# A mixture-of-experts stage: late loads, the place of a branch, gathers by chunk, routing in token halves

## The chip, the core and the metric

One core of a Trainium2 chip runs the whole program. The metric is the device time of one execution in microseconds. TensorE (PE) multiplies matrices and transposes, VectorE (DVE), ScalarE (ACT) and GpSimd (POOL) do the elementwise work, and SyncE (SP) issues nearly all transfers. All numbers are float32.

## The reference

Two transformer blocks follow each other on 256 tokens of width 1024. The first block's mixture of experts is where the change lies:

```python
logits = (xt @ w_router + b_router)                     # 256 x 32
top_vals, top_idx = lax.top_k(logits, 4)
gates = softmax(top_vals)
# for each token and each of its 4 experts e:
hgu  = xb @ w_up_gate[e] + b_up_gate[e]                 # 1024 x 2048
glu  = minimum(hgu[:, :1024], 7.0); lin = clip(hgu[:, 1024:], -7, 7)
hact = glu * sigmoid(1.702 * glu) * (lin + 1.0)
y   += gate * (hact @ w_down[e] + b_down[e])            # 1024 x 1024
# then, on the same rows (ple):
gate = sigmoid(rmsnorm(x) @ w_ple_gate)
x    = x + (p @ w_ple_proj) * gate
```

Ahead of it stand two kinds of attention (`mixer`), behind it a second block (`mixer2`, `ffn2`).

## The kernel before

`moe` keeps both blocks of 128 tokens in `xt` and gives each expert 64 slots. `route` computes the logits, the top 4 of each token and its slot in each expert (`posm`). `turn_half` transposes half of the columns of `xt` for both token blocks into `rT`, by `turn_quarter`; the products with `wr` (L1070) stand in `p4`, go to `l4`, and are turned to tokens in `pr` (L1078). VectorE finds the top 4 (L1085 to L1094), a product with a triangle (`pp`, L1097) counts the slots. `route` is a generator, whose parts `moe` takes one at a time.

For each group of four experts, `select` writes the selection matrix `S` from `posm`, and `gather` multiplies the normalized tokens `hn` with it, chunk by chunk of 128 columns, into `XST`, the experts' inputs, transposed. For each expert `up` multiplies them with the up and gate weights (8 loads of 1 MB, L830), `act` turns the result and applies bias and activation, and `down` multiplies with the down weights (4 loads of 1 MB, L864). `combine_weights` and `combine` bring pairs of experts back to the tokens and add them to `xt`. The loop runs `up(ex)`, then `down(ex - 1)`, so that `act` has time. The orders of PE and of SP in this stage are written out by hand (`manual_schedule`); the other engines are ordered by a planner.

The weights go through 20 buffers of 1 MB: two rings of five, five of the six `g` buffers of the pool `big` (`g3` holds `rT` and later every second `XST`), and `ring3` of five. `self.order` lists them in the order of their use; `raw()` takes the next one. SP issues the loads in program order, and a load waits until the buffer's last reader is done. At expert 20 `retire` is set: when `g0` is next, `ple_proj` takes `g0`, `g1` and `g5` out of the order for what ple needs, and loads `p` and `w_ple_proj`. Its products come as a generator, `extra`, one step behind an `up` or at the end of an expert.

64 slots may be too few for an expert. Then `flag` is 1 and `more_tokens` runs all experts over all tokens in a loop; with these inputs the branch (L976) skips it. It stands between experts 28 and 29. Each engine loads the flag into a register (L975) and branches by itself.

`ple` follows the last expert: `ahead_of` loads the first half of `w_ple_gate` and splits it into two float32r parts (`whi` on ACT, L155, `wlo` on DVE, L156), `feat` transposes `xt` (`tr_m`, L248), and `lin` multiplies (L201 to L203).

Of the kernel before, what the change touches and what calls it, by code (L numbers as in the profile page):

```python
# [10 lines left out]
F32 = mybir.dt.float32  # L11
# [25 lines left out]
RING3 = 5  # L37

# [53 lines left out]
class Net:  # L92
# [640 lines left out]
    def moe(self, stop=None):  # L733
# [4 lines left out]
        with ExitStack() as es:  # L738
# [20 lines left out]
            route = self.route(b1, b2, p_h, p_y, p_m, gates, gT, posm, iota, bT, flag)  # L759
            S, SG, XST, CG, Y, H, U = {}, {}, {}, {}, {}, {}, {}  # L760
            extra = []

# [16 lines left out]
            def gather(g, k2, first=False):  # L779

                flat = lambda t: t.rearrange("p e s -> p (e s)")
                ps = None if first else p_m.tile([P, 2, G, SLOTS], F32, name="pg", tag="m")
                for kk in range(2):
                    k = 2 * k2 + kk
                    o = p_m.tile([P, G, SLOTS], F32, name="pg1", tag="m") if first else ps[:, kk]
                    for b in range(2):
                        nc.tensor.matmul(flat(o), hn[:, b, blk(k)], flat(S[g][b]), start=b == 0 and (first or kk == 0), stop=b == 1, skip_group_check=True)  # L787
                    if first:
                        turn_out(g, k, o, kk)
                if not first:  # L790
                    if k2 % 2:
                        gain = self.gc[:, GFFN + 2 * k2:GFFN + 2 * k2 + 2].unsqueeze(2).to_broadcast([P, 2, G * SLOTS])
                        nc.vector.tensor_tensor(XST[g][:, 2 * k2:2 * k2 + 2].rearrange("p k e s -> p k (e s)"), ps.rearrange("p k e s -> p k (e s)"), gain, op=ALU.mult)
                    else:
                        for kk in range(2):
                            turn_out(g, 2 * k2 + kk, ps[:, kk], 0)
# [59 lines left out]
            def down(ex):  # L856

                hT = H.pop(ex)
                py = p_y.tile([P, 512], F32, name="py", tag="y")
                for k in range(8):  # L860
                    if k % 2 == 0:
                        raw = self.rows_of(a["w_down"][0, ex][k * P:k * P + 256], 2)
                    for n in range(2):
                        nc.tensor.matmul(py[n * 64:n * 64 + 64], hT[:, k], raw[:, k % 2, half(n)], start=k == 0, stop=k == 7, skip_group_check=True)  # L864
                if ex % 2 == 0:
                    Y[ex // 2] = b1.tile([P, 2, 512], F32, name="yy")
                y = Y[ex // 2][ex % 2 * 64:ex % 2 * 64 + 64]
                nc.scalar.copy(y[:, 0], py[0:64])  # L868
                nc.vector.tensor_copy(y[:, 1], py[64:128])

            def down_bias():

                for n in range(2):
                    for b in range(2):
                        po = p_m.tile([P, 512], F32, name="pbd", tag="m")
                        nc.tensor.matmul(po, gT[:, blk(b)], bd[:, half(n)], start=True, stop=True)
                        s = xt[:, b, half(n)]
                        nc.vector.tensor_tensor(s, s, po, op=ALU.add)
# [10 lines left out]
            with tc.manual_schedule(engines={mybir.EngineType.PE, mybir.EngineType.SP}):  # L889
# [4 lines left out]
                gather(0, 0, True)  # L894
# [31 lines left out]
            self.more_tokens(flag, posm, gates, hn, b1, b2, p_up, p_m)  # L926
            with tc.manual_schedule(engines={mybir.EngineType.PE, mybir.EngineType.SP}):
                for ex in range(29, 32):
                    up(ex)
                    if ex == 31:  # L930
                        act(ex)
                    down(ex - 1)
                    if ex < 31:
                        act(ex)
                    if ex == 30:
                        combine(14)
# [8 lines left out]
    def ple_proj(self, p_m):  # L945

        nc, a = self.nc, self.a
        self.retire = None
        self.pj = self.big.tile([P, 2, D], F32, name="pj", tag="g0")
        p = self.big.tile([P, 4, 512], F32, name="p", tag="g1")  # L950
        p, pT = (p[:, i].rearrange("p (b d) -> p b d", b=2) for i in range(2))
        self.order = [o for o in self.order if o[1] not in ("g0", "g1", "g5")]
        nc.sync.dma_start(p, a["p"][0, 0].rearrange("(b p) d -> p b d", p=P))
        raw = self.rows_of(a["w_ple_proj"][0], 2)

        def steps():
# [12 lines left out]
            yield  # L969
        return steps()  # L970

    def more_tokens(self, flag, posm, gates, hn, b1, b2, p_up, p_m):
# [3 lines left out]
        with tc.If(more > 0):  # L976
# [5 lines left out]
            ha = b1.tile([P, 8, T], F32, name="ha", tag="xst")  # L982
# [48 lines left out]
    def turn_quarter(self, n, b, pool, tag):  # L1031
# [5 lines left out]
        nc.vector.tensor_copy(self.rT[:, 4 * n:4 * n + 4, blk(b)], ps)  # L1037

    def route(self, b1, b2, p_h, p_y, p_m, gates, gT, posm, iota, bT, flag):
        nc, a, tc, xt = self.nc, self.a, self.tc, self.xt  # L1040
        with ExitStack() as es:
# [22 lines left out]
            for n in range(2):  # L1064
                if n == 1:
                    for b in range(2):
                        self.turn_quarter(1, b, p_m, "m")
# [6 lines left out]
            l4 = b1.tile([P, T], F32, name="l4", tag="SG0")  # L1074
            nc.vector.tensor_copy(l4, p4)
# [19 lines left out]

            pp = p_m.tile([P, 2, 32], F32, name="pp", tag="m")
# [17 lines left out]

            pb = p_y.tile([P, 4, P], F32, name="pb", tag="y")
            for c in range(4):
                nc.tensor.transpose(pb[:, c], braw[:, blk(c)], self.ident)
            nc.scalar.copy(bT, pb)
            pgt = p_m.tile([32, T], F32, name="pgt", tag="m")
            for b in range(2):  # L1120
                nc.tensor.transpose(pgt[:, blk(b)], gates[:, b], self.ident)
            nc.scalar.copy(gT, pgt)
# [666 lines left out]
```

## Time and profile before

| what | value |
|---|---|
| time, median of 3 runs | 1584.93 us (1582.86 to 1586.02) |
| time of the profiled execution | 1583.55 us |
| its span, first to last instruction | 1581.7 us |
| TensorE busy | 1477.2 us (93%) |
| VectorE, ScalarE, GpSimd busy | 657.1, 457.2, 103.0 us |
| moved by DMA | 499.51 MB, mean 316 GB/s |
| mean granted TensorE clock | 0.993 of full |

The profile is one execution. The share of busy time is a mean over stages with different limits; of a stage one asks what its last wait is for. The granted clock is the part of full speed (2.4 GHz) that TensorE was given in a stretch; 0.50 is 1.2 GHz. Lines are those of the kernel before.

### The profile page before, as it was taken

What the parts mean: (1) busy time and instruction counts of PE and PEld (TensorE: products, weight loads), DVE (VectorE), ACT (ScalarE), POOL (GpSimd) and SP (SyncE); (2) the same over time, 40 slices, a digit from 0 to 9 for tenths busy, and PEclk for the clock granted to TensorE, in tenths of its full rate; (3) what the DMA queues carried; (4) which work ended last, traced back from release to release, by engine and by line L of the source; (5) the groups of instructions that cost most, each with busy time, mean ns of one, the idle gap of its engine ahead of it and who ended that gap; (6) DMA issues with size and microseconds to landing.
All of it is one profiled execution on the core that took longest, in us unless ns stands there. A gap on an engine that the chain in (4) does not pass through costs nothing. (4 is left out here: it accounts for less than half of the span.)

```text
span 1581.7 us, 19461 instructions
## 1 busy us (share of the span) xinstructions
PE 1477.2 (93%) x7671; PEld 839.9 (53%) x7671; DVE 657.1 (42%) x1200; ACT 457.2 (29%) x849; POOL 103.0 (7%) x213
## 2 busy tenths in 40 slices
PE   8999999999998988988998988788999999999998
PEld 6776433333332332332332332222797779899986
DVE  6666313231322222221311231122789657676654
ACT  7655101110100100100110100001677565464443
POOL 3220000000000000000000000000306100000000
PEclk9999999999999999999999999899999999999999
DMA  8737799999999999999999999999354224656651
GB/s 271 299 132 285 284 411 424 423 421 424 423 421 424 423 422 423 424 422 422 392 381 422 421 423 421 421 375 416 129 196 147 81 94 160 195 165 187 187 192 48
DMA packets 135873, 499.51 MB, mean 316 GB/s; under 512 B 12355, under 2 KB 36291, under 8 KB 103011
## 3 DMA queue, kind: packets, MB, share of 16 engines
q1 hardware_dynamic: 135299, 497.31, 79.9%
q8 instruction: 62, 1.02, 0.3%
q10 hardware_dynamic: 480, 0.92, 0.2%
q14 instruction: 32, 0.26, 0.0%
HBM read 497.15 MB, written 1.05 MB: 315 GB/s over the span
## 5 line engine op out<-in xcount | busy, mean ns | idle before, releaser
L830 PE MATMUL pu<-raw,xst 128*64 128x512 f32 x2048 | 459.2, 599 | 26.0 <-DMA raw<-in_w_up_gate_dram 19.5
L830 PEld LDWEIGHTS pu<-raw,xst 128*64 128x64 f32 x2048 | 141.2, 137 | 325.9 <-issue 266.7
L864 PE MATMUL py<-raw,hT 128*64 128x512 f32 x1024 | 238.9, 599 | 40.7 <-DMA raw<-in_w_down_dram 40.5
L156 DVE TENSOR_TENSOR wlo<-raw,whi 128x1024 fp32r<-128x1024 f32 (+2 forms) x178 | 214.9, 1211 | 121.0 <-ACT whi L155 120.6
L155 ACT CAST whi<-raw 128x1024 fp32r<-128x1024 f32 (+2 forms) x178 | 181.0, 1022 | 171.0 <-PE pt_lin L229 83.5
L833 DVE COPY u<-pu 128x512 f32<-128x512 f32 x32 | 22.1, 691 | 419.4 <-PE pu L830 419.4
L229 PE MATMUL pt_lin<-xl,whi 128*128 128x256 f32 x640 | 180.4, 284 | 0.0
L228 PE MATMUL pt_lin<-xh,whi 128*128 128x256 f32 x640 | 179.8, 285 | 0.6 <-ACT xh L257 0.6
L230 PE MATMUL pt_lin<-xh,wlo 128*128 128x256 f32 x640 | 178.7, 283 | 0.4 <-DVE wlo L156 0.4
L864 PEld LDWEIGHTS py<-raw,hT 128*64 128x64 f32 x1024 | 69.5, 136 | 206.1 <-issue 145.8
L846 DVE TENSOR_TENSOR h<-ph,bT 128x512 f32<-128x512 f32 x64 | 44.1, 689 | 256.3 <-PE ph L843 255.5
L832 ACT COPY u<-pu 128x512 f32<-128x512 f32 x32 | 18.8, 586 | 391.1 <-PE pu L830 391.1
L228 PEld LDWEIGHTS pt_lin<-xh,whi 128*128 128x128 f32 x640 | 120.2, 189 | 4.6 <-issue 3.3
L230 PEld LDWEIGHTS pt_lin<-xh,wlo 128*128 128x128 f32 x640 | 120.4, 189 | 4.1 <-issue 3.1
L229 PEld LDWEIGHTS pt_lin<-xl,whi 128*128 128x128 f32 x640 | 121.0, 189 | 2.7 <-issue 2.6
L868 ACT COPY yy<-py 64x512 f32<-64x512 f32 x32 | 18.5, 579 | 280.7 <-PE py L864 280.7
L885 PE MATMUL po<-yy,cg 128*128 128x512 f32 x128 | 62.8, 614 | 9.7 <-DVE xt L887 9.0
L787 PE MATMUL pg<-S,hn 128*128 128x256 f32 x256 | 63.7, 394 | 0.9 <-DVE S L770 0.9
L850 ACT ACTIVATE sg<-h 128x256 f32<-128x256 f32 x64 | 26.7, 417 | 124.2 <-DVE h L848 124.2
L776 POOL TENSOR_TENSOR SG<-S,gates 128x256 f32<-128x256 f32 x16 | 10.9, 703 | 718.1 <-DVE h L848 712.1
L202 PE MATMUL ps_lin<-wlo,xh 128*128 128x512 f32 (+1 forms) x144 | 56.5, 396 | 0.6 <-DVE wlo L156 0.6
L203 PE MATMUL ps_lin<-whi,xl 128*128 128x512 f32 (+1 forms) x144 | 55.4, 389 | 0.0
(449 smaller groups left out, 1744.2 us busy)
## 6 DMA issues: line engine op xcount, KB each, us to landing
raw<-in_w_up_gate_dram SPq DMA_DIRECT2D x256, 1024.0 KB, 19.5
raw<-in_w_down_dram SPq DMA_DIRECT2D x138, 1024.0 KB, 19.7
raw<-in_w_in_dram SPq DMA_DIRECT2D x33, 1024.0 KB, 5.2
raw<-in_w_gate_up_dram SPq DMA_DIRECT2D x44, 512.0 KB, 4.9
raw<-in_w_out_dram SPq DMA_DIRECT2D x8, 1024.0 KB, 13.4
raw<-in_w_ple_gate_dram SPq DMA_DIRECT2D x4, 1024.0 KB
raw<-in_w_ssd_proj_dram SPq DMA_DIRECT2D x4, 1024.0 KB, 4.9
raw<-in_w_in_dram SPq DMA_DIRECT2D x4, 512.0 KB
```

What stands on the lines that cost most here:

```text
L155: a = self.nc.scalar.copy(hi, src)
L156: b = self.nc.vector.tensor_tensor(lo, src, f32(hi), op=ALU.subtract)
L202: nc.tensor.matmul(ps[b][:, :n], xh[:, k, xs], lo[:, c, :n], start=False, stop=False)
L203: i = nc.tensor.matmul(ps[b][:, :n], xl[:, k, xs], hi[:, c, :n], start=False, stop=k == nk - 1)
L228: nc.tensor.matmul(o, hi[:, c, cs], xh[:, k, :], start=k == 0 and j % 2 == 0, stop=False, skip_group_check=True)
L229: nc.tensor.matmul(o, hi[:, c, cs], xl[:, k, :], start=False, stop=False, skip_group_check=True)
L230: nc.tensor.matmul(o, lo[:, c, cs], xh[:, k, :], start=False, stop=k == nk - 1, skip_group_check=True)
L787: nc.tensor.matmul(flat(o), hn[:, b, blk(k)], flat(S[g][b]), start=b == 0 and (first or kk == 0), stop=b == 1, skip_group_check=True)
L830: nc.tensor.matmul(ps[j][q * 64:q * 64 + 64], xst[:, k, i], raw[:, half(2 * q + j)], start=k == 0, stop=k == 7, skip_group_check=True)
L846: nc.vector.tensor_tensor(h, ph, bT[:, :, o:o + 3:2].unsqueeze(3).to_broadcast([P, 4, 2, SLOTS]), op=ALU.add)
L864: nc.tensor.matmul(py[n * 64:n * 64 + 64], hT[:, k], raw[:, k % 2, half(n)], start=k == 0, stop=k == 7, skip_group_check=True)
L885: nc.tensor.matmul(po, CG[c][:, blk(b)], Y[c][:, n], start=True, stop=True)
```

## The change

- **Routing in token halves**: the second half of the columns is transposed, multiplied and copied for one block of 128 tokens after the other; the copies of the second block are shared by ACT and DVE.
- **Between the top 4 and the slot count** PE gets the transposes of the up bias (`braw`), which stood behind `up(0)`, and four products (`WARM`) whose result nobody reads.
- **Gathers by chunk**: group 0 gathers two chunks ahead of `up(0)` (four before) and one chunk ahead of each of its products 1 to 6 (two chunks ahead of two of them before). `combine_weights(0)`, `select(1)` and `gather(1, 0)` move from behind `act(0)` into expert 1, and the rest of group 1's gathers into experts 2 and 3.
- **Late loads into retired slots**: `w_ple_proj` goes to `g5`, `p` to `g1`, `b_down` to a free part of `g1`. `b_down` was loaded ahead of the experts, its product with the gates (`down_bias`) stood behind `act(0)`; both move to `ple_proj`, as two more steps.
- **The branch** moves from between experts 28 and 29 to behind the last `combine`; behind the first products of `down(31)` PE is given a hint that it will be taken. The tile `ha` of the skipped part moves to `g3`.

```diff
@@ moe
-            gT = b1.tile([32, T], F32, name="gT", tag="cg2")
-            bd = b1.tile([32, D], F32, name="bd", tag="yy")
-            nc.scalar.dma_start(bd, a["b_down"][0])
...
+            def gather1(k):
+
+                o = p_m.tile([P, G, SLOTS], F32, name="pg1", tag="m")
+                for b in range(2):
+                    nc.tensor.matmul(flat(o), hn[:, b, blk(k)], flat(S[0][b]), start=b == 0, stop=b == 1)
+                turn_out(0, k, o, k % 2)
...
-                        nc.tensor.matmul(py[n * 64:n * 64 + 64], hT[:, k], raw[:, k % 2, half(n)], start=k == 0, stop=k == 7, skip_group_check=True)
+                        i = nc.tensor.matmul(py[n * 64:n * 64 + 64], hT[:, k], raw[:, k % 2, half(n)], start=k == 0, stop=k == 7, skip_group_check=True)
+                    if k == 0:
+                        self.mm = i.ins
...
                 select(0)
-                gather(0, 0, True)
+                gather1(0)
+                gather1(1)
                 next(route)
                 select_gates(0)
 
-                up(0, lambda k: gather(0, k // 2 + 1, True) if k in (0, 2, 4) else None)
+                up(0, lambda k: gather1(k + 1) if 0 < k < 7 else None)
                 next(route)
                 act(0)
-                down_bias()
-                combine_weights(0)
-                select(1)
-                gather(1, 0)
-                for ex in range(1, 29):
+                for ex in range(1, 32):
                     g, i = ex // G, ex % G
                     if ex == 20:
-                        self.retire = lambda: extra.append(self.ple_proj(p_m))
+                        self.retire = lambda: extra.append(self.ple_proj(p_m, gates))
                     up(ex)
                     if extra:
                         next(extra[0], None)
+                    if ex == 31:
+                        act(ex)
                     down(ex - 1)
-                    act(ex)
+                    if ex < 31:
+                        act(ex)
+                    if ex == 1:
+                        combine_weights(0)
...
-                        if i == 0:
+                        if i == (1 if g == 0 else 0):
                             select(g + 1)
-                        gather(g + 1, i)
+                        for k2 in [i] if g else {1: [0], 2: [1], 3: [2, 3]}[i]:
+                            gather(g + 1, k2)
...
-            self.more_tokens(flag, posm, gates, hn, b1, b2, p_up, p_m)
-            with tc.manual_schedule(engines={mybir.EngineType.PE, mybir.EngineType.SP}):
-                for ex in range(29, 32):
...
                 down(31)
+                with tc.issue_after(self.mm):
+                    tc.mark_branch_hint_location("more", "LikelyTaken", [mybir.EngineType.PE])
                 combine(15, True)
             self.order = []
+            self.more_tokens(flag, posm, gates, hn, b1, b2, p_up, p_m)
@@ ple_proj
-        p = self.big.tile([P, 4, 512], F32, name="p", tag="g1")
...
+        t = self.big.tile([P, 4, 512], F32, name="p", tag="g1")
...
+        bd = t[0:32, 2:4].rearrange("p a f -> p (a f)")
+        raw = self.big.tile([P, 2, D], F32, name="wpj", tag="g5")
+        nc.sync.dma_start(raw, a["w_ple_proj"][0].rearrange("(c p) f -> p c f", p=P))
         nc.sync.dma_start(p, a["p"][0, 0].rearrange("(b p) d -> p b d", p=P))
-        raw = self.rows_of(a["w_ple_proj"][0], 2)
+        nc.sync.dma_start(bd, a["b_down"][0])
...
             yield
+            ps = p_m.tile([32, T], F32, name="pgt", tag="m")
+            for b in range(2):
+                nc.tensor.transpose(ps[:, blk(b)], gates[:, b], self.ident)
+            gT = p[0:32, 0]
+            nc.scalar.copy(gT, ps)
+            yield
+            for n in range(2):
+                for b in range(2):
+                    po = p_m.tile([P, 512], F32, name="pbd", tag="m")
+                    nc.tensor.matmul(po, gT[:, blk(b)], bd[:, half(n)], start=True, stop=True)
+                    s = xt[:, b, half(n)]
+                    nc.vector.tensor_tensor(s, s, po, op=ALU.add)
+            yield
@@ more_tokens
-        with tc.If(more > 0):
+        with tc.If(more > 0, label="more"):
...
-            ha = b1.tile([P, 8, T], F32, name="ha", tag="xst")
+            ha = self.big.tile([P, 8, T], F32, name="ha", tag="g3")
@@ turn_quarter
+        if both:
+            nc.scalar.copy(self.rT[:, 4 * n:4 * n + 2, blk(b)], ps[:, :2])
+        o = 2 if both else 0
+        nc.vector.tensor_copy(self.rT[:, 4 * n + o:4 * n + 4, blk(b)], ps[:, o:])
@@ route
+            def logits(n, b):
                 for j in range(4):
                     k = 4 * n + j
-                    nc.tensor.matmul(p4[j * 32:j * 32 + 32], self.wr[:, k], rT[:, k], start=n == 0, stop=n == 1, skip_group_check=True)
+                    nc.tensor.matmul(p4[j * 32:j * 32 + 32, blk(b)], self.wr[:, k], rT[:, k, blk(b)], start=n == 0 and b == 0, stop=n == 1, skip_group_check=True)
+
+            self.turn_quarter(1, 0, p_m, "m")
+            logits(0, 0)
+            logits(0, 1)
+            self.turn_quarter(1, 1, p_m, "m", True)
+            logits(1, 0)
+            nc.scalar.copy(l4[:, blk(0)], p4[:, blk(0)])
+            logits(1, 1)
+            nc.vector.tensor_copy(l4[:, blk(1)], p4[:, blk(1)])
...
+            pw = p_y.tile([P, T], F32, name="pwarm", tag="y")
+            for k in range(WARM):
+                nc.tensor.matmul(pw, self.ident, rT[:, k], start=True, stop=True)
```

## Rows read from the trace of the kernel before

**Rows 1.** The page's slices: GB/s in 40 equal parts of the span.

```profile
...
GB/s 271 299 132 285 284 411 424 423 421 424 423 421 424 423 422 423 424 422 422 392 381 422 421 423 421 421 375 416 129 196 147 81 94 160 195 165 187 187 192 48
...
```

**Rows 2.** Windows of the expert stage; columns: us, busy time by engine, granted clock, DMA, GB/s.

```profile
...
165.00:203.00 38.00, 37.54 (x166) 16.94 (x166) 10.48 (x23) 6.44 (x13) 1.38 (x2) 0.98 0.71 272
203.00:785.00 582.00, 541.58 (x2416) 197.68 (x2412) 143.33 (x303) 53.32 (x113) 6.98 (x10) 1.00 1.02 423
785.00:796.00 11.00, 11.00 (x37) 4.77 (x38) 4.23 (x11) 3.18 (x6) 0.00 (x0) 1.00 0.44 166
...
1034.00:1044.00 10.00, 9.81 (x50) 3.62 (x48) 4.67 (x11) 1.42 (x3) 0.00 (x0) 1.00 0.63 233
1044.00:1100.00 56.00, 46.98 (x200) 14.54 (x200) 12.98 (x28) 3.99 (x8) 0.00 (x0) 1.00 1.02 420
...
```

**Rows 3.** Waits of PE in the whole span: us in total, times, longest.

```profile
...
PE py L864 <- DMA raw<-in_w_down_dram: 40.5, 71, 2.0
...
```

**Rows 4.** Timeline of the SP queue, 165 to 215 us.

```profile
...
169.89 16.49 SPq L135 DMA_DIRECT2D raw<-in_w_up_gate_dram  x8
196.63 5.52 SPq L135 DMA_DIRECT2D raw<-in_w_down_dram  x4
...
```

**Rows 5.** Timeline of PE, 176 to 204 us.

```profile
...
178.93 7.09 PE L830 MATMUL pu<-raw,xst 128*64 128x512 f32 x32
185.94 0.66 PE L1117 MATMUL pb<-ident,braw 128*128 128x128 f32 x4
...
187.73 3.95 PE L876 MATMUL pbd<-bd,gT 32*128 32x512 f32 x8
...
192.79 1.93 PE L787 MATMUL pg<-S,hn 128*128 128x256 f32 x8
194.65 9.66 PE L830 MATMUL pu<-raw,xst 128*64 128x512 f32 x44
```

**Rows 6.** Timeline of the routing, 138 to 204 us, all engines.

```profile
...
153.85 1.09 PE L1036 MATMUL ptr<-ident,xt 128*128 128x128 f32 x8
...
154.86 1.28 DVE L1037 COPY rT<-ptr 128x512 f32<-128x512 f32 x2
...
160.47 0.66 PE L1097 MATMUL pp<-wide,ustr 128*128 128x64 f32 x2 [2.46 <-DVE wide L1094]
...
162.37 5.61 PE L787 MATMUL pg<-S,hn 128*128 128x256 f32 x16 [0.87 <-DVE S L770]
...
```

**Rows 7.** Windows of 1 us; the granted clock is third from last.

```profile
...
160.00:161.00 1.00, 0.54 (x3) 0.57 (x3) 0.36 (x3) 0.53 (x2) 0.00 (x0) 0.50 1.02 410
...
1015.00:1016.00 1.00, 1.00 (x4) 0.26 (x2) 0.00 (x0) 0.00 (x0) 0.00 (x0) 0.50 1.02 418
...
```

**Rows 8.** Waits of the SP queue, 780 to 800 us.

```profile
...
SPq L135 <- PE ppj L967: 19.1, 1, 19.1
...
```

**Rows 9.** Line 976, the branch: instructions by engine, ns, start; who waited.

```profile
...
L976 SPq EVENT_SEMAPHORE  x8: 17/17/17, 1026.7 to 1039.1; - x8
...
L976 PEldq COMPARE_BRANCH  x1: 5932/5932/5932, 1004.1 to 1004.1; - x1
...
L976 DVEq COMPARE_BRANCH  x1: 72/72/72, 1004.8 to 1004.8; - x1
...
  DVE hT L853: 1.0, 1
...
```

**Rows 10.** Timeline of DVE behind the last expert, 1102 to 1108 us.

```profile
...
1104.62 1.22 DVE L156 TENSOR_TENSOR wlo<-raw,whi 128x1024 fp32r<-128x1024 f32 x1
1105.76 1.87 DVE L887 TENSOR_TENSOR xt<-xt,po 128x512 f32<-128x512 f32 x3
...
```

**Rows 11.** Timeline of PE at the end of the stage, 1078 to 1122 us.

```profile
...
1100.24 1.94 PE L864 MATMUL py<-raw,hT 128*64 128x512 f32 x8 [0.46 <-DMA raw<-in_w_down_dram]
1102.86 3.70 PE L885 MATMUL po<-yy,cg 128*128 128x512 f32 x8 [0.68 <-ACT yy L868]
1106.39 1.04 PE L248 MATMUL tr_m<-ident,xt 128*128 128x128 f32 x8
...
```

More of the change, by code (lines that the diff above doesn't have):

```diff
@@ L758, in moe @@
             self.order = (old[:5] + [g[2]] + old[5:7] + [g[0], g[1], g[4]] + old[7:8] + [g[5]] + old[8:] + [(ring3, "raw")] * RING3) * 40
-            route = self.route(b1, b2, p_h, p_y, p_m, gates, gT, posm, iota, bT, flag)
+            route = self.route(b1, b2, p_h, p_y, p_m, gates, posm, iota, bT, flag)
             S, SG, XST, CG, Y, H, U = {}, {}, {}, {}, {}, {}, {}
             extra = []
+            flat = lambda t: t.rearrange("p e s -> p (e s)")
             def select(g):
@@ L777, in select_gates, with gather @@
                                             gates[:, b, es_].unsqueeze(2).to_broadcast([P, G, SLOTS]), op=ALU.mult)
-            def gather(g, k2, first=False):
-                flat = lambda t: t.rearrange("p e s -> p (e s)")
-                ps = None if first else p_m.tile([P, 2, G, SLOTS], F32, name="pg", tag="m")
+            def gather(g, k2):
+                ps = p_m.tile([P, 2, G, SLOTS], F32, name="pg", tag="m")
                 for kk in range(2):
-                    k = 2 * k2 + kk
-                    o = p_m.tile([P, G, SLOTS], F32, name="pg1", tag="m") if first else ps[:, kk]
                     for b in range(2):
[L787 to L796, printed above, removed]
+                        nc.tensor.matmul(flat(ps[:, kk]), hn[:, b, blk(2 * k2 + kk)], flat(S[g][b]), start=b == 0 and kk == 0, stop=b == 1, skip_group_check=True)
+                if k2 % 2:
+                    gain = self.gc[:, GFFN + 2 * k2:GFFN + 2 * k2 + 2].unsqueeze(2).to_broadcast([P, 2, G * SLOTS])
+                    nc.vector.tensor_tensor(XST[g][:, 2 * k2:2 * k2 + 2].rearrange("p k e s -> p k (e s)"), ps.rearrange("p k e s -> p k (e s)"), gain, op=ALU.mult)
+                else:
+                    for kk in range(2):
+                        turn_out(g, 2 * k2 + kk, ps[:, kk], 0)
+            def gather1(k):
[3 more added lines that the diff above has]
+                turn_out(0, k, o, k % 2)
             def turn_out(g, k, o, on):
@@ L869, in down @@
                 nc.vector.tensor_copy(y[:, 1], py[64:128])
[L871 to L878, printed above, removed]
             def combine(c, last=False):
@@ L943, in moe, with ple_proj @@
                 self.ple((b1, b2, ((p_y, "y"), (p_up, "pu")), p_m))
-    def ple_proj(self, p_m):
-        nc, a = self.nc, self.a
+    def ple_proj(self, p_m, gates):
+        nc, a, xt = self.nc, self.a, self.xt
         self.retire = None
+        self.order = [o for o in self.order if o[1] not in ("g0", "g1", "g5")]
         self.pj = self.big.tile([P, 2, D], F32, name="pj", tag="g0")
-        p = self.big.tile([P, 4, 512], F32, name="p", tag="g1")
-        p, pT = (p[:, i].rearrange("p (b d) -> p b d", b=2) for i in range(2))
-        self.order = [o for o in self.order if o[1] not in ("g0", "g1", "g5")]
+        t = self.big.tile([P, 4, 512], F32, name="p", tag="g1")
+        p, pT = (t[:, i].rearrange("p (b d) -> p b d", b=2) for i in range(2))
+        bd = t[0:32, 2:4].rearrange("p a f -> p (a f)")
+        raw = self.big.tile([P, 2, D], F32, name="wpj", tag="g5")
+        nc.sync.dma_start(raw, a["w_ple_proj"][0].rearrange("(c p) f -> p c f", p=P))
         nc.sync.dma_start(p, a["p"][0, 0].rearrange("(b p) d -> p b d", p=P))
-        raw = self.rows_of(a["w_ple_proj"][0], 2)
+        nc.sync.dma_start(bd, a["b_down"][0])
         def steps():
@@ L1094, in route @@
             nc.vector.tensor_tensor(sel, eq, gt, op=ALU.add)
+            pb = p_y.tile([P, 4, P], F32, name="pb", tag="y")
+            for c in range(4):
+                nc.tensor.transpose(pb[:, c], braw[:, blk(c)], self.ident)
+            nc.scalar.copy(bT, pb)
+            pw = p_y.tile([P, T], F32, name="pwarm", tag="y")
+            for k in range(WARM):
+                nc.tensor.matmul(pw, self.ident, rT[:, k], start=True, stop=True)
             pp = p_m.tile([P, 2, 32], F32, name="pp", tag="m")
@@ L1113, in route @@
             yield
[L1115 to L1122, printed above, removed]
             ps = p_m.tile([1, P], F32, name="pom", tag="m")
```

21 lines of the change are left out of this document (4 added, 17 removed).

## The prediction

> **What bounds the kernel now.** I read the page's slices first: they say where the span is full and with what [rows 1]. From about 200 to 1100 us every slice moves some 420 GB/s, except three (392, 381 and 375) that hold short holes; left and right of that stretch the transfers run far below. This is the expert stage: 32 experts of 12 MB of weights each, through 20 buffers of 1 MB. Second, the windows of that stage [rows 2]: 423 GB/s from 203 to 785 and 420 up to the last weight, so 423 is what this stream reaches, and 1 MB (1.049 million bytes) takes 2.48 us. TensorE is not far behind: it is busy 541.6 of 582 us there. Third, who waits for whom [rows 3]: the longest of TensorE's waits is for weights of the down projection, 40.5 us in 71 pieces. So the transfers bound the stage, TensorE follows them with at least 40 us to spare, and the end of the stage is bytes divided by 423 GB/s plus every hole in the stream. A hole filled is paid back at the end in full, as long as nothing behind it becomes the bound.
>
> There are three holes [rows 2]. At the head, 165 to 203 us, 272 GB/s: 38 x (1 - 272/423) = 13.6 us missing. At 785 to 796, 166 GB/s: 11 x (1 - 166/423) = 6.7 us. At 1034 to 1044, 233 GB/s: 10 x (1 - 233/423) = 4.5 us. The change touches the cause of each.
>
> **The head hole.** 20 buffers are full at 165 us, and the next load waits until expert 0's matmuls give a buffer back. The SP queue shows it [rows 4]: eight loads go out from 169.89 on, at the pace of expert 0's up projection, then none until 196.63, when expert 1's first chunk is done. So what counts is when `up(1)` starts; it started at 194.65 [rows 5].
>
> First part, routing. Before, eight transposes of 1.09 us in all, two copies of 1.28 us, the logits and their copy stand in line [rows 6]. In halves, only the second token block's four transposes (0.55 us less), one copy instead of two (0.64 less) and half of it on ScalarE (0.32 less) remain on the path; 1.5 us, of which I take 1.4 for a ScalarE that has a sum of squares ahead of its half. Then TensorE waits 2.46 us, up to 160.47, for VectorE's top-4 [rows 6], and from there the granted clock is 0.50, the 1.2 GHz level [rows 7]. The change puts the transposes of `braw` (0.66 us [rows 5]) and four warming products into that gap: four products of 128x256 are eight instructions, as a later gather's 1.93 us group [rows 5], together 2.59 against a gap of 2.46 us, so 0.1 us late. If the clock then stays at 2.4 GHz, the 16 gather instructions, 5.61 us and mostly at the low clock [rows 6], take 2 x 1.93 = 3.86: 1.7 us, and the prefix product's 0.66 us half of it: 0.3. Sum: 1.4 - 0.1 + 1.7 + 0.3 = 3.3 us. Gathering by single chunks lets the first product of expert 0 start after two chunks instead of four, another 2 us earlier; the total up to `up(1)` stays, but the first buffers come free earlier. If the clock falls all the same, 2.0 of the 3.3 are gone.
>
> Second part, what stood between the two up projections. From 185.94 to 194.65 TensorE ran transposes, the bias product (3.95 us), gate transposes and a gather [rows 5]: 8.7 us that free no buffer. After, the flag's transpose and expert 0's eight transposes remain, the second half waiting for VectorE's copy: about 1.4 us. Gain 7.3 us, and bounds 7.0 to 7.7 (the transposes without that wait).
>
> So `up(1)` comes 10.6 us earlier, near 184. Can the loads follow? The eight loads ahead need 8 x 2.48 = 19.8 us from about 165.5 on, so they end near 186, just when expert 1's first buffer is free. In `up(0)` a buffer comes free every 1.77 us (7.09 for four chunks) plus 0.97 for a chunk's gather (half of 1.93) [rows 5], 2.74 against 2.48, which leaves a small hole. I take 10.6; bounds 7 (no routing gain) and 12. What moves into experts 1 to 3 (combine weights, the gather of chunks) is the same work later, under the 40 us of slack.
>
> **The hole at 785.** SP waits 19.1 us for the product `ppj` [rows 8]: the weight of the ple projection sat in a ring buffer, and the ring came round to it before TensorE had used it. The loads in flight cover most of the wait, 6.7 us of the stream are lost. After, it goes to `g5`, which the ring has dropped, so nobody waits for it. Its own wait is for what `g5` held 16 loads earlier, consumed long before. Cost: `b_down` (0.13 MB) now rides in the full stream, 0.3 us. The bias product (3.95 us [rows 5]) and the gate transposes land on TensorE here, under its slack; without that cover they would cost over 4. Gain 6.4, bounds 0 (the wait stays) and 6.7.
>
> **The branch.** Today it stands before expert 29. TensorE's compare-and-branch took 5932 ns, VectorE's 72 [rows 9]. On SP eight semaphore instructions follow, the last at 1039.1 [rows 9]: it takes up its queue only when all loads in flight have landed, and that is the 4.5 us hole. TensorE's wait was under its slack. Behind the last expert no expert load stands behind the drain: gain 4.5 us.
>
> But now the drain and the branch are in the tail, where nothing covers them. The ple gate's weights, today directly behind the last expert's, start when SP has drained: 4.5 us later at most. Their first split has its VectorE half at 1104.62 [rows 10]. With the last expert weight at 1100.24 (where the last products of `down(31)` end their wait [rows 11]), the first ple weight arrives some 4.6 to 7 us after it, about when VectorE has got through the branch. VectorE: the first split (1.22 us [rows 10]) can no longer sit between the additions to `xt`, and the flag load and branch cost about 1 us (today's first work behind the branch waited 1.0 [rows 9]) after the last of them, which ends near 1107.6 [rows 10]. The first transpose of ple came at 1106.39, at the end of the combine products [rows 11], and will wait for that. Sum 1.0 + 1.2 = 2.2; I take 2.5. Lower bound 0 (all overlaps). Upper bound: the hint does nothing; then 5.9 us of branch on TensorE, from the end of the combine at 1106.56, and a start at half clock: after today's branch the clock was 0.50 still at 1015 [rows 7], six busy us, 3 us lost. That is about 10.
>
> The Trainium skill ("Runtime: NRT & Kernel Launch", section "Instruction fetch mechanics") says that a taken branch whose target lies outside the fetched window stalls for a fetch by DMA, and advises against runtime control flow; the 5932 ns beside 72 ns [rows 9] agrees. By that rule alone the tail would have the upper bound and the sum would be -11.5; no row here shows what a hint does.
>
> **Sum.** -10.6 - 6.4 - 4.5 + 2.5 = -19.0. The profiled execution took 1583.55 us (span 1581.7 and 1.85 around it), which gives 1564.6; it is 1.4 below the median of 1584.93, so I say **1565**.
>
> **Rivals.**
> 1. The hint does not hold: tail 10 instead of 2.5, so 1572. For it: the only branch measured cost 5932 ns under full transfers. Against: the hint is given behind the first products of the last down projection, with three more loads of 2.48 us and the combine (3.70 us [rows 11]) still to come, over 11 us.
> 2. TensorE's clock falls in the routing anyway: 2.0 us less at the head and a slower start of `up(0)`, some 1 us: 1568. For it: the warming products fill the gap of 2.46 us, not the shorter ones before it.
> 3. One fill does not reach the end: SP still waits at 785 or finds a new wait for `g5`; 6.4 us back: 1571. Against: the ring has 17 buffers left and some eight loads in flight.
> 4. Slower: instruction fetch in the tail. The branch skips the largest body of the kernel; if the hinted fetch throws out what TensorE is about to run, each miss costs 5.9 us and keeps the clock low. At four misses (24 us) the gain of 21.5 is gone: 1588. For it only the one miss; against, that a single miss was all that the old place cost.
> 5. No change, the bound being TensorE after all: the filled holes would appear as waits for buffers. TensorE would have to lose its 40 us; the moved work is some 4. About 1584.
>
> **How the numbers follow.** Forecast 0.68, rival 1 0.13, rival 2 0.07, rival 3 0.05, rival 4 0.04, rival 5 0.03. The range takes the bounds of head and tail: 1565 - 4 (head 12, tail 0) - 3 for a deeper fill than the windows show and the spread of runs (3.2 us here) gives 1558; rival 1 with a part of rival 2 gives 1576. No change means within 0.2%, 3.2 us, about what a measurement here can tell. Faster 0.92 (forecast, rivals 1 to 3, less a little), same 0.03, slower 0.05.
>
> **What would show it.** `up(1)` near 184 and the first load behind it near 186; granted clock 1.00 at 160 to 166. No SP wait for `ppj`; 423 GB/s from 186 to the last expert weight, which lands near 1079. A branch of well under 1 us on TensorE and 2 to 3 us between the last combine product and ple's first product beyond today's. Wrong would be: a 5 us idle stretch of TensorE behind the combine, a new hole near 785, or the stream at 423 with TensorE the one that others wait for.

## The result: 1568.65 us, 1.0% faster

The changed kernel took a median of 1568.65 us (1567.39 to 1570.17, 6 runs), the kernel before 1585.32 us beside it (1582.86 to 1586.02, 6 runs): ratio 0.9898, 95% interval 0.9885 to 0.991. The median lies inside the forecast's range of 1558 to 1576 and 3.65 us above the forecast of 1565. The profiled execution took 1567.39 us (span 1565.6), 1.3 us less than its median.

The transfer row of the page's slices, in GB/s; the three slices that held holes [rows 1], the 20th, 21st and 27th, are at 422, 421 and 423; the 19th, at 413, holds a new dip:

```profile
GB/s 277 297 135 278 365 423 423 423 423 424 421 422 424 423 422 423 422 423 413 422 421 422 421 422 422 422 423 392 94 183 133 84 92 162 198 167 189 189 197 44
```

The windows of the expert stage in the changed kernel:

```profile
165.00:203.00 38.00, 37.84 (x172) 14.04 (x172) 7.73 (x19) 4.71 (x8) 0.00 (x0) 1.00 0.97 377
...
738.00:743.00 5.00, 4.28 (x20) 1.99 (x20) 1.66 (x4) 0.58 (x1) 0.00 (x0) 1.00 1.04 362
...
785.00:796.00 11.00, 11.00 (x54) 3.73 (x52) 0.00 (x0) 0.00 (x0) 0.00 (x0) 1.00 1.01 416
...
1034.00:1044.00 10.00, 7.87 (x36) 2.29 (x35) 0.69 (x1) 0.06 (x1) 0.00 (x0) 1.00 1.02 426
```

Where 272, 166 and 233 GB/s stood [rows 2] there are 377, 416 and 426. The new dip is shallow: 362 GB/s over 5 us where the late loads (`w_ple_proj`, `p`, `b_down`) pass. Of SP's wait for `ppj`, 19.1 us [rows 8], the list of waits still has 1.7 us (L959); the 416 GB/s at 785 to 796 say that it costs the stream next to nothing. TensorE's longest wait for a load is still that for the down weights, now 34.4 us [rows 3].

TensorE at the head of the stage, start and duration, and SP's loads there:

```profile
157.09 1.89 PE L1117 MATMUL pwarm<-rT,ident 128*128 128x256 f32 x8
...
160.71 1.97 PE L796 MATMUL pg<-S,hn 128*128 128x256 f32 x8 [0.87 <-DVE S L770]
162.60 1.94 PE L831 MATMUL pu<-raw,xst 128*64 128x512 f32 x8
164.47 1.13 PE L796 MATMUL pg<-S,hn 128*128 128x256 f32 x4
...
183.75 0.27 PE L1139 MATMUL pom<-ident,om 128*1 128x128 f32 x1
...
185.21 1.08 PE L831 MATMUL pu<-raw,xst 128*64 128x512 f32 x4
```

```profile
164.58 19.61 SPq L137 DMA_DIRECT2D raw<-in_w_up_gate_dram  x8
187.19 5.52 SPq L137 DMA_DIRECT2D raw<-in_w_down_dram  x4
```

`up(1)` starts at 185.21 instead of 194.65 [rows 5], and the first load that waits for it goes out at 187.19 instead of 196.63 [rows 4].

The end of the stage on TensorE (last weight's products, combine, ple), and the new branch (L981), with its duration on TensorE's sequencer in ns:

```profile
1081.72 1.94 PE L865 MATMUL py<-raw,hT 128*64 128x512 f32 x8 [0.45 <-DMA raw<-in_w_down_dram]
...
1084.33 3.70 PE L879 MATMUL po<-yy,cg 128*128 128x512 f32 x8 [0.68 <-ACT yy L871]
...
1090.10 1.06 PE L250 MATMUL tr_m<-ident,xt 128*128 128x128 f32 x8 [2.06 <-DVEq L981]
...
1091.18 0.55 PE L203 MATMUL ps_y<-whi,plexh 128*128 128x512 f32 x1
```

```profile
L981 SPq EVENT_SEMAPHORE  x8: 17/17/17, 1092.0 to 1097.8; - x8
...
L981 PEldq COMPARE_BRANCH  x1: 481/481/481, 1085.7 to 1085.7; - x1
```

The last products of `down(31)` come at 1081.72, 18.5 us earlier than 1100.24 [rows 11]. TensorE's branch takes 481 ns, not 5932 [rows 9]. Then it waits 2.06 us for VectorE, and that wait is followed by half clock in this execution:

```profile
1092.00:1093.00 1.00, 1.00 (x4) 0.81 (x3) 0.92 (x3) 0.93 (x3) 0.00 (x0) 0.50 0.66 254
```

Below, "the stream is so much later" means: the same number of bytes has been moved that much later than in the profile of the changed kernel, read from its DMA records. The edits are shown condensed. Each experiment was timed beside the kernel before; an interval is about 0.0015 to either side of a ratio, some 2.3 us, so two experiments closer than that are told apart by the trace alone.

### The profile page after: what moved, and what is told of

The parts are those of the page before. It is cut to its first block, busy times and chain, and to the rows that moved or that the text cites. A ratio compares the mean times of both kernels' runs of the same rounds, so it can differ in the third digit from the quotient of the medians.

```text
span 1565.6 us, 19525 instructions
## 1 busy us (share of the span) xinstructions
PE 1474.6 (94%) x7695; PEld 838.4 (54%) x7695; DVE 657.7 (42%) x1200; ACT 457.3 (29%) x851; POOL 103.0 (7%) x213
## 3 DMA queue, kind: packets, MB, share of 16 engines
HBM read 497.15 MB, written 1.05 MB: 318 GB/s over the span
## 5 line engine op out<-in xcount | busy, mean ns | idle before, releaser
L865 PE MATMUL py<-raw,hT 128*64 128x512 f32 x1024 | 238.0, 598 | 34.5 <-DMA raw<-in_w_down_dram 34.4
L871 ACT COPY yy<-py 64x512 f32<-64x512 f32 x32 | 18.5, 579 | 272.4 <-PE py L865 272.4
L784 PE MATMUL pg<-S,hn 128*128 128x256 f32 x224 | 54.0, 385 | 0.2 <-ACT cg L813 0.2
```

What stands on the lines that cost most here:

```text
L784: nc.tensor.matmul(flat(ps[:, kk]), hn[:, b, blk(2 * k2 + kk)], flat(S[g][b]), start=b == 0 and kk == 0, stop=b == 1, skip_group_check=True)
L865: i = nc.tensor.matmul(py[n * 64:n * 64 + 64], hT[:, k], raw[:, k % 2, half(n)], start=k == 0, stop=k == 7, skip_group_check=True)
```

## The experiments

| kernel | median us (range) | ratio (interval) |
|---|---|---|
| the change | 1568.65 (1567.39 to 1570.17) | 0.9898 (0.9885 to 0.991) |
| branch back, no hint | 1571.07 (1569.43 to 1573.61) | 0.9908 (0.9893 to 0.9923) |
| no hint | 1570.57 (1569.38 to 1571.23) | 0.9907 (0.9892 to 0.9923) |
| branch back, other queue | 1571.03 (1569.0 to 1572.53) | 0.9909 (0.9893 to 0.9924) |
| no warming | 1570.22 (1568.68 to 1573.25) | 0.9909 (0.9896 to 0.9923) |
| `w_ple_proj` in the ring | 1574.49 (1571.68 to 1575.55) | 0.9936 (0.9921 to 0.995) |
| `b_down` four times | 1571.43 (1570.11 to 1573.32) | 0.992 (0.9905 to 0.9934) |
| gathers in pairs | 1568.44 (1566.61 to 1568.63) | 0.9901 (0.9883 to 0.9918) |
| bias product early | 1576.54 (1574.24 to 1578.29) | 0.995 (0.9935 to 0.9965) |
| whole-block routing | 1569.49 (1567.18 to 1570.76) | 0.9904 (0.9889 to 0.9918) |
| four chunks ahead | 1568.91 (1566.2 to 1570.99) | 0.9897 (0.9881 to 0.9913) |
| warming in the tail | 1570.84 (1569.61 to 1572.04) | 0.9915 (0.9901 to 0.9929) |
| the same, later hint | 1570.4 (1569.4 to 1571.99) | 0.9907 (0.9892 to 0.9922) |

**1. The ring's hole.**

```diff
-        raw = self.big.tile([P, 2, D], F32, name="wpj", tag="g5")
-        nc.sync.dma_start(raw, a["w_ple_proj"][0]...)
+        raw = self.rows_of(a["w_ple_proj"][0], 2)
```

> The changed kernel with one part undone: the weight of the ple projection is loaded through a ring buffer again, as before, all else as in the change. Theory (the ring came round to that weight before TensorE had used it): SP waits some 15 to 20 us for the projection near 775, the stream falls below 200 GB/s for about 11 us there, and everything behind is 6 to 6.7 us later: about 1575. Rival (with the head's hole gone TensorE is earlier relative to the ring, or the gain at 785 came from something else in the change): no SP wait for it, 423 GB/s through, and the time of the change, 1568 to 1569.

SP's wait and a window in place of the one that was filled:

```profile
SPq L137 <- PE ppj L958: 19.1, 1, 19.1
```

```profile
780.00:791.00 11.00, 11.00 (x37) 4.12 (x37) 2.77 (x7) 2.76 (x5) 0.00 (x0) 1.00 0.43 165
```

The wait is 19.1 us as before the change [rows 8], the stream goes from 1.3 to 8.45 us late there, and the median is 5.8 us longer. The theory holds: one buffer's choice is worth its whole hole.

**2. What stood between the two up projections.**

```diff
+            nc.scalar.dma_start(bd, a["b_down"][0])   # ahead of the stage
                 act(0)
+                # gate transposes, four products pbd, additions to xt
```

> The changed kernel with the bias product and the transposes of the gates back between the first two up projections, b_down loaded ahead of the stage on ScalarE's queue and no longer in the stream. Theory (TensorE's work between the two up projections sets when the loads of expert 1's pace begin): the second up projection starts 4.3 us later than 185.2, the stream is 4.3 us later from there, less 1.0 us for the load that leaves the stream: 3.3 us longer in all, 1572. Rival (the loads in flight cover a part of it, or the gain at the head came from the routing alone): within 1 us of the change, 1568 to 1569.5.

TensorE between the two up projections, and the window behind it:

```profile
186.83 1.98 PE L906 MATMUL pbd<-bd,gT 32*128 32x512 f32 x4 [0.45 <-ACT gT L902]
190.41 3.78 PE L906 MATMUL pbd<-bd,gT 32*128 32x512 f32 x4 [1.60 <-DVE xt L908]
194.12 12.39 PE L834 MATMUL pu<-raw,xst 128*64 128x512 f32 x50
```

```profile
190.00:199.00 9.00, 8.59 (x20) 2.73 (x22) 3.40 (x8) 0.42 (x1) 0.00 (x0) 0.62 0.06 13
```

`up(1)` comes 8.9 us later, 0.9 of it from ahead of the stage: 8.0, not 4.3. The third product waits 1.60 us for VectorE, and the granted clock is 0.62 from 190 to 199 us. The transfers stand at 13 GB/s for 9 us. The first load that waits for `up(1)` goes out 3.42 us after its start, not 1.98, since its first products run at the low clock too. The stream is 10.4 us later behind the head, 9.4 at the end (the late dip is gone: 1.0), the median 7.9 us longer. So the theory's mechanism holds, the stream follows `up(1)` in full; only its price of the work was half of what it is.

**3. The warming products.**

```diff
-WARM = 4
+WARM = 0
```

> The changed kernel with no warming products (WARM = 0). Theory (they keep the clock up over the wait for the top 4): granted clock 0.50 in the first gathers, expert 1's up projection 2 to 3 us later, 1571 us. Rival (the shorter gaps of the routing in halves and the moved transposes do it alone): clock 1.00, 1568 to 1569 us.

TensorE and two of the windows at the gathers:

```profile
160.81 3.59 PE L796 MATMUL pg<-S,hn 128*128 128x256 f32 x8 [0.87 <-DVE S L770]
164.33 1.94 PE L831 MATMUL pu<-raw,xst 128*64 128x512 f32 x8
```

```profile
161.00:162.00 1.00, 1.00 (x3) 0.82 (x4) 0.42 (x3) 0.00 (x0) 0.36 (x1) 0.50 0.99 393
162.00:163.00 1.00, 1.00 (x4) 0.81 (x3) 0.00 (x0) 0.10 (x1) 0.82 (x2) 0.50 1.07 430
```

The clock falls to 0.50, the first gathers take 3.59 instead of 1.97 us, and everything up to ple is 1.7 to 2.0 us later (the median 1.6 us). The mechanism holds, at 1.6 us for the gathers.

**4. Routing in halves.**

```diff
-            self.turn_quarter(1, 0, p_m, "m"); logits(0, 0); logits(0, 1)
-            self.turn_quarter(1, 1, p_m, "m", True); logits(1, 0); logits(1, 1)
+            # both blocks' transposes, then all products of the second half, one copy
```

> The changed kernel with the routing in whole token blocks as before: eight transposes and two copies, then all the logits and one copy on VectorE; the warming products and all else stay. Theory (the halves shorten the path to the top-4 by 1.4 us): the logits' last product to the scores and all that follows come 1 to 1.5 us later, the second up projection too, 1570. Rival (the gap that the halves fill is paid at another place, or the head is bound by the loads in flight): within 0.5 us of the change, 1568.5 to 1569.

The first transposes and the slot count (`pp`), first in the changed kernel, then in this one:

```profile
150.78 1.03 PE L1042 MATMUL ptr<-ident,xt 128*128 128x128 f32 x8
...
159.23 0.41 PE L1120 MATMUL pp<-wide,ustr 128*128 128x64 f32 x2 [0.26 <-DVE wide L1109]
```

```profile
150.44 1.03 PE L1042 MATMUL ptr<-ident,xt 128*128 128x128 f32 x8
...
159.69 0.41 PE L1115 MATMUL pp<-wide,ustr 128*128 128x64 f32 x2 [0.25 <-DVE wide L1104]
```

From the first transpose to the slot count it took 9.25 us instead of 8.45. So the halves are worth 0.8 us, between theory and rival; the medians differ by as much, which is less than they can tell.

**5. Gathers.** In pairs behind the first two chunks, and, in a second kernel, four chunks ahead as before the change:

```diff
-  up(0, lambda k: gather1(k + 1) if 0 < k < 7 else None)
+  up(0, lambda k: (gather1(k + 1), gather1(k + 2)) if k in (1, 3, 5) else None)
+  up(0, lambda k: (gather1(k + 2), gather1(k + 3)) if k in (0, 2, 4) else None)
```

> The changed kernel with expert 0's later gathers made in pairs of chunks, as before the change, but the first two chunks still singly. Theory (each single gather costs 1.06 us of TensorE against 0.97 for half a pair, and a switch of products more): the second up projection starts about 0.5 to 1 us earlier than 185.2 and the time is 0.5 to 1 us shorter, 1568. Rival (the buffers' times decide, and a pair gives back one buffer later than a single chunk): the loads of the head are issued later and the time is the same or 0.5 us longer.

> The changed kernel with expert 0's gathers as before the change: four chunks ahead of the first product, then two pairs. Theory (what counts is when buffers come free, and the second up projection's start stays): the first product comes 2 us later, the first load of the head too, the second up projection starts up to 1 us earlier than 185.2, and the loads that wait in between cost the stream 1 to 2 us: 1569.5 to 1570.5. Rival (the second up projection alone sets the stream behind the head): 1568 or less.

The start of `up(1)`, first with pairs, then with four ahead:

```profile
183.92 13.95 PE L831 MATMUL pu<-raw,xst 128*64 128x512 f32 x64
```

```profile
183.88 0.65 PE L831 MATMUL pu<-raw,xst 128*64 128x512 f32 x2
```

`up(1)` came 1.05 us earlier with pairs and 1.4 with four ahead (against the same start of the stage). The stream came no earlier: 0.6 and 1.9 us later. With four ahead SP's first load goes out late, and the window behind it is emptier than the changed kernel's 334 GB/s:

```profile
166.37 16.49 SPq L137 DMA_DIRECT2D raw<-in_w_up_gate_dram  x8
```

```profile
165.00:177.00 12.00, 12.00 (x56) 5.29 (x54) 1.66 (x4) 0.95 (x2) 0.00 (x0) 1.00 0.73 274
```

In the medians neither differs from the change. The trace speaks for the buffers' times, but the stream also shifts by chance here: of the seven other profiles with the change's code at the head (experiments 1, 6, 7, 8 and 9) six lost 0.9 to 1.5 us more than the change's own between 177 and 205 us. What gathering by chunk brings is 1 us or less, and not settled.

**6. The price of a load on 32 partitions.**

```diff
+  for i in range(1, 4):
+      nc.sync.dma_start(t[i*32:i*32+32, 2:4]..., a["b_down"][0])
```

> The changed kernel with three more copies of the load of b_down (32 partitions of 4 KB, 0.13 MB each), into the other three groups of partitions of the same part of g5; nothing reads them. Theory (a load on 32 partitions costs the full stream about 1.0 us, not the 0.3 us of its bytes): the stretch near 740 falls below 380 GB/s for longer, the stream is 3 us later from there on, and the time 1571.5. Rival (it costs its bytes alone): 0.9 us in all, 1569.5. If the four copies together fill all the DMA engines evenly where one alone did not, also nearer the second.

```profile
735.00:745.00 10.00, 8.07 (x36) 3.05 (x36) 1.57 (x3) 0.58 (x1) 0.00 (x0) 1.00 1.05 341
745.00:755.00 10.00, 8.74 (x36) 3.54 (x34) 5.87 (x13) 2.31 (x6) 1.39 (x2) 1.00 1.01 390
```

The copies go to `g1`, where `b_down` is; the expectation's `g5` is a slip. By the count of all bytes the stream is 1.9 us late ahead of the copies and 3.7 us late behind them: 1.8 us, and that count has the copies' own 0.39 MB as bytes moved. The weights wait for these too, 0.9 us at 423 GB/s, so three copies cost the weights 2.7 to 2.8 us, 0.9 each: three times what the bytes take, and close to the theory's 1.0. The median is 2.8 us longer. The theory holds, the rival (bytes alone) does not. The last weight's products start 5.1 us later than in the change: 1.9 from ahead of the copies, 2.8 from them; the remaining 0.4 is open.

**7. The branch's place.** Back between experts 28 and 29, without the hint; and there with the hint, with the skipped part's transfers on ScalarE's queue:

```diff
+  for ex in range(1, 29): expert(ex)
+  self.more_tokens(...)
+  for ex in range(29, 32): expert(ex)
```

```diff
-            nc.sync.dma_start(gd, gm)      # and four more in more_tokens
+            nc.scalar.dma_start(gd, gm)
```

> The changed kernel with only the branch put back between experts 28 and 29, without a hint. Theory (the time is the holes in the weight stream plus the uncovered tail): the hole of 4.5 us comes back into the stream, TensorE's branch wait of some 6 us stays under its slack, and the tail's 3.8 us (2.25 of waiting, 1.55 of half clock) go; net +0.7, 1569 to 1570 us, and ple's first product again 7.2 us behind the last expert weight. Rival (moving the branch was worth its 4.5 us of stream or TensorE's 6.4 us): 1573 to 1575 us.

> The branch between experts 28 and 29, with a hint at the first products of that expert's down projection, and the transfers of the skipped part issued by ScalarE instead of SP. Theory (the hole at the old place was SP waiting for its loads in flight, because the skipped part has transfers of its own queue): SP passes the branch without a wait, the stream has no hole, the tail is as before the change; 3.8 us less than the changed kernel, 1564 to 1566 us. Rival (the hole belongs to the branch itself): the 4.5 us hole stays, 1569 to 1570 us.

SP's branch window in the first kernel, and TensorE's first ple product there:

```profile
1014.00:1027.00 13.00, 13.00 (x66) 5.75 (x64) 3.59 (x8) 1.58 (x3) 0.00 (x0) 1.00 0.63 264
```

```profile
1096.23 0.50 PE L203 MATMUL ps_y<-whi,plexh 128*128 128x512 f32 x1 [1.22 <-ACT plexh L259]
```

SP's semaphores, TensorE's branch and the same window in the second:

```profile
L987 SPq EVENT_SEMAPHORE  x8: 17/17/17, 1014.1 to 1026.6; - x8
L987 PEldq COMPARE_BRANCH  x1: 6067/6067/6067, 991.7 to 991.7; - x1
```

```profile
1014.00:1027.00 13.00, 13.00 (x66) 4.65 (x62) 4.94 (x11) 2.00 (x4) 0.00 (x0) 1.00 0.67 281
```

In the first the stream loses 6.5 us at the branch, and the tail (last weight to the first `ps_pu`) is 2.8 us shorter, and the last weight's products lag the stream 1.1 us less; with 0.7 from ahead of the branch that makes 3.3 us at ple, and 2.4 in the median, between theory and rival. So the theory has the right parts but not their sizes (4.5 and 3.8 us). One part it missed: ple's first product came 8.4 us behind the last expert weight, not 7.2, because TensorE now waited 1.22 us for ScalarE, which ran three splits in a row ahead of its first copy of `tr_m`. Of the 2.25 us that the tail lost by the order of work, the branch's old place gave back only 1.05. In the second SP executes the same eight semaphores while its loads land, and the hole is about 6 us: whose queue the skipped transfers are on does not matter. That theory fell. And the hint did nothing there (6067 ns).

**8. The hint.**

```diff
-  with tc.issue_after(self.mm):
-      tc.mark_branch_hint_location("more", "LikelyTaken", [mybir.EngineType.PE])
```

> The changed kernel without the branch hint. Theory (the hint fetched the target ahead): TensorE's compare-and-branch takes 5.9 us again instead of 0.48, behind the last combine product, where nothing covers it, and the clock is low for longer: 5 to 8 us more, 1574 to 1577 us. Rival (the branch is short because of its new place): no change, 1568 to 1570 us.

```profile
L979 PEldq COMPARE_BRANCH  x1: 5992/5992/5992, 1085.7 to 1085.7; - x1
```

The branch takes 5992 ns from 1085.7, under the combine products and VectorE's part; what reaches ple is 2.44 us at its first product and 1.7 at `ps_pu`. The truth lies between: the hint saves 5.5 us of branch and some 1.7 us of time.

**9. Warming in the tail,** against the half clock behind the branch; then with the hint four products later:

```diff
+  pw = p_up.tile([P, T], F32, name="pwarm2", tag="pu")
+  for k in range(4):
+      nc.tensor.matmul(pw, self.ident, hn[:, 0, k*T:k*T+T], start=True, stop=True)
```

```diff
+  if k == 2: self.mm2 = i.ins      # in down
-  with tc.issue_after(self.mm):
+  with tc.issue_after(self.mm2):
```

> The changed kernel with four more products (128x128 by 128x256, into a buffer that nothing reads) between the last combine product and the branch on TensorE, some 1.9 us of work in the 2.06 us in which TensorE waits for the flag. Theory (the wait lets the clock fall to the 1.2 GHz level at 1091 to 1095, and that costs about 1.5 us): the granted clock stays at 1.00 there, the first ple product comes at most 0.2 us later, the ple stage ends 1.3 to 1.6 us earlier, and the time is 1567. Rival (the ple stage is bound by the splits of its weights, and the slow products are covered): the clock stays up and the time is that of the change, 1568 to 1569.

> The kernel with four warming products ahead of the branch, in which TensorE's branch took 6038 ns though it was hinted at, with the hint four products later, behind the sixth product of the last down projection instead of the second. Between hint and branch then stand 18 products, as in the changed kernel where the branch took 481 ns, instead of 22 (6038 ns); 30 stood there in the kernel with the branch between experts 28 and 29 (6067 ns). Theory (a hint holds for a limited number of instructions behind it): the branch takes 0.5 us again, the clock stays at 1.00 through 1091 to 1095, ple's stage ends 1.3 to 1.6 us earlier than in the changed kernel with the same stream, and the time is 1567 to 1567.5. Rival (something else decides, the place of the code in memory for one): the branch takes 6 us again and the time is 1570 to 1571. Third case (the hint now comes some 9 us ahead of the branch and that is too short for what it fetches): the branch takes between 0.5 and 6 us.

The first kernel's branch took 6 us, though hinted at as far ahead (11.3 us) as in the change:

```profile
L984 PEldq COMPARE_BRANCH  x1: 6038/6038/6038, 1087.2 to 1087.2; - x1
```

The DMA queues between hint and branch show the difference (packets, MB, share). First the changed kernel, 1075 to 1085.6 us, then this one, 1076 to 1087.1:

```profile
q1 hardware_dynamic: 1811, 4.30, 103.2%
q8 instruction: 1, 0.02, 0.6%
```

```profile
q1 hardware_dynamic: 1854, 4.50, 103.4%
```

In the change one 16 KB packet of instructions arrives some 8.5 us behind the hint and 2.8 us ahead of the branch; so it is in all eight hinted profiles whose branch took 481 to 486 ns. Here, as in the hinted kernel of experiment 7, none comes until 3.6 us after the branch has begun, as without a hint. The later hint (9.1 us ahead) gave 5205 ns:

```profile
L986 PEldq COMPARE_BRANCH  x1: 5205/5205/5205, 1086.2 to 1086.2; - x1
```

The packet came 2.7 us after this branch had begun, 0.9 us sooner than where the hint did nothing. So 18 products between hint and branch are not enough by themselves (18 worked, 22 did not, 18 again did not). But this hint also stood 2.2 us nearer to the branch, and 5205 ns is what the third case had: neither the number of products nor a hint that comes too late is ruled out, and what decides is open. In that last kernel the clock did hold:

```profile
1088.20 1.89 PE L931 MATMUL pwarm<-hn,ident 128*128 128x256 f32 x8
...
1091.73 1.06 PE L250 MATMUL tr_m<-ident,xt 128*128 128x128 f32 x8 [1.63 <-PEq L986]
```

```profile
1094.00:1095.00 1.00, 1.00 (x6) 0.79 (x5) 0.98 (x2) 0.71 (x2) 0.00 (x0) 1.00 0.70 258
```

From ple's first product to its first `ps_pu` it took 11.07 us, against 12.15 in the change; the branch takes that back. That the warming held the clock is not shown: in experiments 1, 2 and 5 (pairs) it stayed at 1.00 there without such products. No version beat the change by more than can be measured.

## Why the prediction was right

The forecast's case came about. (By its own sum the forecast for the median is 1584.93 - 19.0 = 1565.9, not 1565.) These are the terms (the profiled executions, span 1581.7 to 1565.6 us; minus is earlier):

| term | forecast | in the trace |
|---|---|---|
| ahead of the stage | 0 | -0.4 |
| head hole | -10.6 | -8.9 |
| hole at 785 | -6.7 | -6.7 |
| late loads in the stream | +0.3 | +1.0 |
| branch hole | -4.5 | -4.7 |
| last weight behind the stream | 0 | +1.3 |
| tail, order of work | +2.5 | +2.25 |
| tail, half clock | 0 | +1.5 |
| second block, clock | 0 | -1.4 |
| sum | -19.0 | -16.1 |

The stream's rows count all bytes. Before the change `b_down`'s 0.13 MB (0.3 us) were in that count from the start; for the weights alone the head is -9.2 and the late loads +1.3.

**Bound.** Right: the transfers bound the stage and holes come back in full, shown in both directions by experiments 1 and 2. Rival 5 is out.

**Head: right in mechanism, 1.6 us too large.** `up(1)` came 9.0 us earlier (9.44 less the 0.4 from ahead of the stage) instead of 10.6. The step that failed is "the total up to `up(1)` stays": in `up(0)` a chunk with its gather takes 2.93 us (164.47 to 167.40), not 2.74, and single chunks put `up(1)` 1.4 us later than four chunks ahead (experiment 5). The halves brought 0.8 instead of 1.4 (experiment 4). The clock was sized about right: from the slot count to the end of `up(0)` the kernel with four chunks ahead took 2.3 us less than the kernel before, where the sum had 2.0; leaving out the warming products alone costs 1.6 of it with single chunks (experiment 3). Between the two up projections the 1.4 us left were right: 1.46 from `pom` to `up(1)`. So `up(1)` stands at 185.2, not 184.

**Hole at 785: right.** **`b_down`: mis-sized,** 1.3 us for the weights instead of 0.3, which was its bytes alone; experiment 6 gives 0.9 for one such load.

**Branch and tail: right for the most part.** The hole is filled, the hint held, and the tail's order of work cost 2.25 us. That the hint held was luck as far as the prediction's reason goes, a lead of over 11 us: the first kernel of experiment 9 had the same lead, and its branch took 6038 ns. The sentence that the ple gate's weights start when SP has drained was wrong: they were issued at 1066.41, ahead of the branch, and SP's eight semaphores held up only `mixer2`'s loads. The upper bound (10 us without the hint) was far too high; measured, 1.7 us more, because TensorE's branch ran under the combine products and VectorE's part (experiment 8).

**Not foreseen.** The last weight's products lag the stream by 4.25 us where they lagged 2.94, counted from the same byte. In the two kernels with the branch's hole back in the stream it was 3.0 to 3.15, in the others 3.65 to 4.9 (in experiment 6 without the bytes of the copies); why is open. The half clock costs 1.5 us in the profiled execution and is not there in all: from ple's first product to `ps_pu` experiments 1, 2 and 5 (pairs), with the same code there, took 10.62, as before the change. And the second block won 1.4 us that are chance: at the start of `ffn2` the profile before has the clock at 0.56, the one after at 1.00, on the same work. From the first `ps_pu` to the end five of the fourteen profiles took 461.9 to 462.3 us and nine 463.6 to 465.3, with the same code there. First the kernel before, then the change:

```profile
1388.00:1390.00 2.00, 2.00 (x13) 2.00 (x12) 1.73 (x4) 1.32 (x5) 0.00 (x0) 0.56 0.00 0
```

```profile
1374.00:1376.00 2.00, 2.00 (x20) 2.00 (x19) 1.82 (x5) 0.85 (x3) 0.00 (x0) 1.00 0.00 0
```

This and the favourable head (experiment 5) may be why the profiled execution lies 1.3 us below the median. Rival 2 did not come (clock 1.00 at 160 to 164), rival 3 neither; of rival 4 there is no trace, the stretch behind the branch holding one short wait. The rule cited from the Trainium skill ("Runtime: NRT & Kernel Launch", section "Instruction fetch mechanics"), that a taken branch to a target not yet fetched stalls, agrees with 5932 and 5992 ns unhinted and 481 ns hinted; the sum by that rule alone (-11.5) did not come, since the stall is mostly covered even unhinted.

## What to carry to other kernels

Where transfers bound a stage, look for the holes in the stream, name for each the buffer, the branch or the late product that makes it, and count it in full; but count what the work moved elsewhere costs there, since products beside a slow VectorE or behind an idle gap can cost twice their busy time. A branch hint is no part of the program that can be trusted unseen: look for the instruction packet between hint and branch, and put the branch where a missed hint is covered anyway. Differences of 1 to 2 us need several profiles: the clock and the stream's start vary by that much from one execution to the next.

## What was unexpected of the hardware

- A hinted branch took 481 to 486 ns in eight profiles and 5205 to 6067 ns in three, and only in the eight was there an instruction packet in time.
- SP executes eight semaphore instructions at a branch, 1014.1 to 1026.6 us in experiment 7, even when none of the skipped transfers is SP's; the loads behind them wait.
- A load of 0.13 MB on 32 partitions cost the weights of a full stream 0.9 us, three times what its bytes take at 423 GB/s.
- Four products whose result nobody reads (1.89 us), put into TensorE's wait for the top 4, kept the granted clock at 1.00 in all twelve profiles that have them; in experiment 3, without them, it was 0.50 for some 3 us.
